# MoBA's scale, bias and maximum in one VectorE pass, its 1/sum scaling and some copies and fills on GpSimd

## The chip, the core and the metric

One core of one Trainium2 chip runs the whole program. The metric is the device time in microseconds of one execution, as the median of several. PE stands for TensorE, DVE for VectorE, ACT for ScalarE, POOL for GpSimd, SP for SyncE.

## What is computed

A decoder trunk of two layers on 256 tokens of width 1024, in float32. Each layer is a SwiGLU half-step, a mixing step, a cross-attention over 256 memory tokens, and a second SwiGLU half-step. The mixing step projects the normed tokens once and feeds the columns to an RWKV-7 time mix (8 heads of 64) and to MoBA, a block-sparse attention (8 heads of 64). With 256 tokens and blocks of 256 there is only each query's own block, so MoBA is a causal softmax attention with a bias by distance:

```python
s_own = jnp.einsum('bhqd,bhkd->bhqk', q_c, k_own).astype(f32) + bias_own.astype(f32)[None]
s_own = jnp.where(own_pos[None, :] <= q_pos[:, None], s_own, -jnp.inf)
...
probs = jax.nn.softmax(logits, axis=-1).astype(v.dtype)
```

where `q` has been multiplied by 64 ** -0.5 = 0.125.

## The kernel before

Every weight matmul is done in three terms of a high and a low half. `load` (L101) brings 1 MB of weights into one of two `raw` buffers by a DMA from SP's queue; `split` (L85) makes the high half on ACT (tile `whi`) and the low half on DVE (tile `wlo`, a subtraction with two inputs in SBUF), into five buffers each. PE consumes them in groups of 24 matmuls of 256 columns.

`mix` (L878) runs three things against each other: the generator `rwkv` (L560), the generator `moba` (L483), and projections of the memory tokens for the cross-attention (`late`, L928), which are the weight matmuls of this stretch. `rwkv` yields numbers, and `mix` hands out pieces of the others against them; the Tile scheduler then sets the order in which each engine's queue holds its instructions, and each engine works through its queue in that order.

`moba` has the steps `scores(h)` and then `values(h - 1)`, for 8 heads. For each head `scores` puts q k^T into a PSUM bank (`acc`, tile `mqk` as input) in two pieces, `t` = 0 (128 queries by 128 keys) and `t` = 1 (128 by 256). DVE multiplies by 0.125 and adds the bias `bp` (L511), takes the negated maximum (L516), ACT takes the exponential with its row sum (L517), DVE the reciprocal of the sums (L519), and ACT multiplies by it (L521, shown as L83). `values` transposes `lg` on PE in three parts (L530), copies them out on ACT (`mpT`), and multiplies by v. The bias table is made once by `moba_bias` (L472) and loaded per pair of heads by a DMA from POOL's queue (L492).

In `rwkv`, after the products `XB` of each half `cp` of the chunks, 32-row blocks are copied to `UD` (L691, ACT) and 16-row blocks to `UA` (L694, POOL); a transpose (`UT`, L699) and then 14 pairs of a product `pr` (L720) and a sum into `mb` (L722) on DVE invert small triangular matrices. The inverses become `M` and `W2` (L729); PE then multiplies `UA` by `M` (L762), and so on in 32 by 32 pieces. The zero parts of `G` (L613), `W` (L732) and of the first state `SV` (L752) are filled on DVE.

Of the kernel before, what the change touches and what calls it, by code (L numbers as in the profile page):

```python
# [11 lines left out]
AF = mybir.ActivationFunctionType  # L12
OP = mybir.AluOpType
AX = mybir.AxisListType

D = 1024
S = 256
# [9 lines left out]
NEG = -1e30  # L27
# [20 lines left out]
def body(tc, ctx, I, out):  # L48
    nc = tc.nc
# [7 lines left out]
    V = nc.vector  # L57
    A = nc.scalar
# [8 lines left out]
    def H(shape, dt=FT, name="h", tag="e"):  # L67
        return hp.tile(shape, dt, name=nm(name), tag=tag, bufs=HEAP[tag])

    def SM(shape, dt=FT, name="s", tag="sm"):  # L70
        return sp.tile(shape, dt, name=nm(name), tag=tag, bufs=SMALL.get(tag, 8))

    def BANK(tag):
        return ps.tile([128, 512], FT, name=nm(tag), tag=tag, bufs=BANKS[tag])

    def tt(out_, a, b, op):
        V.tensor_tensor(out=out_, in0=a, in1=b, op=op)  # L77

    def stt(out_, a, s, b, op0, op1):
        V.scalar_tensor_tensor(out_, a, s, b, op0=op0, op1=op1)  # L80

    def copy(out_, in_, **k):
        return A.activation(out_, in_, AF.Copy, **k)  # L83

    def split(hi, lo, src):  # L85
        c = copy(hi, src)
        tt(lo, src, hi.bitcast(FT), OP.subtract)
        return c.ins
# [4 lines left out]
    def mm(o, a, b, start=True, stop=True):  # L93
        nc.tensor.matmul(o, a, b, start=start, stop=stop, skip_group_check=True)  # L94
# [377 lines left out]
    def moba_bias():  # L472
        rel, oh = table
        u = SM([8, 384], name="u", tag="k2")
        V.memset(u[:, 256:384], NEG)
        p = BANK("pm")
        mm(p[0:8, 0:S], rel, oh)
        copy(u[:, 0:S], p[0:8, 0:S])
        nc.gpsimd.dma_start(scr_t, u)
        t = scr_t[:, :]  # L480
        nc.gpsimd.dma_start(scr_b, bass.AP(tensor=t.tensor, offset=t.offset, ap=[[0, 128], [1, 8 * 384]]))

    def moba(qT, kT, v, yT):  # L483

        scr = scr_b[:, :]
        cols = (slice(0, 128), slice(128, 384))
        probs, os = {}, {}

        def load_bias(p):
            if p < 4:  # L490
                bias[p] = SM([128, 2, S], name="bp", tag="k3")
                nc.gpsimd.dma_start(bias[p], bass.AP(  # L492
                    tensor=scr.tensor, offset=scr.offset + 2 * p * 384 + 127,
                    ap=[[8 * 384 - 1, 128], [384, 2], [1, S]]))

        bias = {}
        load_bias(0)
        yield 0.0

        def scores(h):  # L500
            p, e = divmod(h, 2)
            r = half(e)
            if e == 0:
                load_bias(p + 1)
            s = BANK("acc")
            for t in range(2):
                mm(s[:, cols[t]], qT[p // 2][r, p % 2, t * 128:(t + 1) * 128],
                   kT[p // 2][r, p % 2, 0:(t + 1) * 128])
            lg = SM([128, 384], name="lg", tag="k3")
            for t in range(2):  # L510
                stt(lg[:, cols[t]], s[:, cols[t]], 0.125, bias[p][:, e, 128 * (1 - t):S],  # L511
                    OP.mult, OP.add)
            m = SM([128, 2], name="m", tag="n2")
            z = SM([128, 2], name="z", tag="n2")
            for t in range(2):
                V.tensor_reduce(m[:, t:t + 1], lg[:, cols[t]], axis=AX.X, op=OP.max, negate=True)  # L516
                A.activation(lg[:, cols[t]], lg[:, cols[t]], AF.Exp, bias=m[:, t:t + 1],  # L517
                             accum_out=z[:, t:t + 1])
            V.reciprocal(z, z)  # L519
            for t in range(2):  # L520
                copy(lg[:, cols[t]], lg[:, cols[t]], scale=z[:, t:t + 1])  # L521
            probs[h] = lg

        def values(h):
            p, e = divmod(h, 2)
            r = half(e)
            lg = probs.pop(h)
            q = BANK("acc")[:, 0:384].rearrange("p (k t) -> p k t", k=3)
            for k in range(3):
                nc.tensor.transpose(q[:, k, :], lg[:, k * 128:(k + 1) * 128], ident)  # L530
            pT = SM([128, 3, 128], name="mpT", tag="k3")
            copy(pT, q)
            if e == 0:
                os[p] = BANK("acc")
            o = os[p]
            for t in range(2):
                for k in range(t + 1):
                    mm(o[r, t * 128:(t + 1) * 128], v[k][:, h * 64:h * 64 + 64], pT[:, t + k, :],
                       k == 0, k == t)
            if e:  # L540
                split(yT[0][:, p, :], yT[1][:, p, :], o[:, 0:S])

        for h in range(9):
            if h < 8:
                scores(h)
            if h:
                values(h - 1)
            yield 1.6
# [8 lines left out]
    def half(e):  # L557
        return slice(e * 64, e * 64 + 64)

    def rwkv(l, xT, yT):  # L560
# [26 lines left out]
        for j in range(2):  # L587
            for which in range(3):
                ac = BANK("pm").rearrange("p (c t) -> p c t", c=2)
                for c in range(2):  # L590
                    p = 2 * j + c
# [5 lines left out]
                for c in range(2):  # L597
                    p = 2 * j + c
                    if which == 2:
                        copy(G1[:, p, :], ac[:, c, :], scale=X(8, p))  # L600
                    else:
                        A.activation((sg, a)[which][:, p, :], ac[:, c, :], AF.Sigmoid,
                                     bias=P((P_W0, P_A0)[which], p))
# [5 lines left out]
        for p in range(4):  # L609
            V.tensor_tensor_scan(Lc[:, p, :], con[:, C_SCAN:C_SCAN + S], sg[:, p, :], 0.0,  # L610
                                 op0=OP.mult, op1=OP.add)
        G = H([128, 4, NCH, 65], name="G")
        V.memset(G[:, :, :, 0:1], 1.0)  # L613
        A.activation(G[:, :, :, 1:65], ch(Lc), AF.Exp, scale=-DECAY_C)
        Gi = H([128, 4, S], name="Gi")
        A.activation(Gi, Lc, AF.Exp, scale=DECAY_C)
# [56 lines left out]
        quads = [slice(32 * b, 32 * b + 32) for b in range(4)]  # L673
        UD = SM([128, 16, 4, 4, 2], name="UD", tag="k2")
        for c in range(NCH):
            cp, cc = divmod(c, 2)
            for e in range(2):
                hs, ho = half(e), half(1 - e)
                px = BANK("pm").rearrange("p (c t) -> p c t", c=4)
                for p in range(4):  # L680
                    mm(px[:, p, :], BK[cp][hs, cc, p, :], ZL[e][cp][hs, cc, p, :])
                tt(XB[cp][hs, cc], px[0:64], con[hs, None, C_MB:C_MB + 128].to_broadcast([64, 4, 128]),
                   OP.mult)
                tt(ZL[e][cp][ho, cc], px[64:128],
                   con[ho, None, C_MK:C_MK + 128].to_broadcast([64, 4, 128]), OP.mult)
                yield XY
            if cc:
                for b in range(4):
                    c0 = (b // 2) * 64 + (b % 2) * 32
                    z = XB[cp][quads[b], :, :, c0:c0 + 32]  # L690
                    copy(UD[quads[b], :, 2 * cp:2 * cp + 2].rearrange("p i n c b -> p (n c) b i"),  # L691
                         z.rearrange("p n c (b i) -> p (n c) b i", b=2))
                    r16 = slice(32 * b, 32 * b + 16)
                    nc.gpsimd.tensor_copy(UA[r16, cp * 8:cp * 8 + 8, 16:32],  # L694
                                          z[0:16, :, :, 16:32].rearrange("p n c t -> p (n c) t"))
# [11 lines left out]
        for c in range(NCH):  # L707
            cp, cc = divmod(c, 2)
# [6 lines left out]
        for i in range(14, -1, -1):  # L715
            n = 15 - i
# [12 lines left out]
            V.transpose(zz.rearrange("p n (b i) -> p i n b", b=2), ex.rearrange("p i b j -> p (i b j)"))  # L729
        W = H([128, 16, 64], name="W")  # L730
        for e in range(2):
            V.memset(W[e * 64 + 32:e * 64 + 64, :, 0:32], 0.0)  # L732
        SV = []
        pvt = []

# [13 lines left out]

        values(0)  # L750
        for e in range(2):
            V.memset(SV[0][half(e), :, e, 0, :], 0.0)  # L752
        hq = [slice(e * 64, e * 64 + 32) for e in range(2)]
        hr = [slice(e * 64 + 32, e * 64 + 64) for e in range(2)]
        for cp in range(2):
# [47 lines left out]
        for c in range(NCH):  # L803
            cp, cc = divmod(c, 2)
# [219 lines left out]
    first, scale = start()  # L1024
    gf = None
    for l in range(L):
        xT = [o[0] for o in ops[4 * l:4 * l + 4]]
        post = [o[1] for o in ops[4 * l + 1:4 * l + 5]]
        ffn(xT[0] if l else xT0, I["w_f1i"][l], I["w_f1o"][l], post[0], I["w_mixb"][l],
            *(() if l else (  # L1030
                {2: (bias_load,), 3: (aux_params,), 4: (mem_tokens,), 7: (moba_bias,), 9: (mem_norm,)}, first, scale)))
        kT, vx = mix(l, xT[1], post[1])
        xattn(l, xT[2], kT, vx, post[2], I["w_f2i"][l])
        if l == L - 1:
            gf = H([128, D], name="gf")
            nc.gpsimd.dma_start(gf, bass.AP(tensor=I["gfin"].tensor, offset=I["gfin"].offset,
                                            ap=[[0, 128], [1, D]]))
            V.tensor_scalar(gf, gf, RS, None, op0=OP.mult)
        ffn(xT[3], I["w_f2i"][l], I["w_f2o"][l], post[3], I["w_f1i"][l + 1] if l < L - 1 else None)
# [116 lines left out]
```

## Time and profile before

| | |
|---|---|
| median of 3 runs | 1313.62 us (1313.3 to 1314.08) |
| the profiled execution | 1309.71 us |
| its span in the trace | 1307.9 us |
| busy: PE, DVE, ACT, POOL | 1290.9, 919.2, 761.8, 63.0 us |
| granted clock of PE, mean | 0.998 |

The span runs from the first to the last instruction of the trace; the device time has 1.8 us around it. The MoBA part of the first layer lies at some 290 to 350 us of the span, that of the second layer at some 936 to 997 us, with the same instructions in the same order on PE. A matmul that starts while the one before it still runs is drawn overlapping, so what PE loses is read from the spacing of the starts as much as from its idle time.

### The profile page before, as it was taken

What the parts mean: (1) busy time and instruction counts of PE and PEld (TensorE: products, weight loads), DVE (VectorE), ACT (ScalarE), POOL (GpSimd) and SP (SyncE); (2) the same over time, 40 slices, a digit from 0 to 9 for tenths busy, and PEclk for the clock granted to TensorE, in tenths of its full rate; (3) what the DMA queues carried; (4) which work ended last, traced back from release to release, by engine and by line L of the source; (5) the groups of instructions that cost most, each with busy time, mean ns of one, the idle gap of its engine ahead of it and who ended that gap; (6) DMA issues with size and microseconds to landing.
All of it is one profiled execution on the core that took longest, in us unless ns stands there. A gap on an engine that the chain in (4) does not pass through costs nothing.

```text
span 1307.9 us, 21991 instructions
## 1 busy us (share of the span) xinstructions
PE 1290.9 (99%) x8710; PEld 1107.2 (85%) x8710; DVE 919.2 (70%) x1703; ACT 761.8 (58%) x1447; POOL 63.0 (5%) x69
## 2 busy tenths in 40 slices
PE   9999999999999999999999999999999999999997
PEld 7888888998878888888888888889887798888886
DVE  6797556797598676665576665658966976777744
ACT  6656437658656466554365554574785555665543
POOL 0080000020000000000000000000200000000000
PEclk9999999999999999999999999999999999999999
DMA  7867663333235335556545556443431455355552
GB/s 283 315 238 251 220 209 129 130 129 117 102 139 193 133 134 199 186 190 223 193 140 184 192 194 225 145 139 120 144 133 66 140 183 173 134 193 192 185 173 95
DMA packets 34422, 224.36 MB, mean 172 GB/s; under 512 B 4328, under 2 KB 4752, under 8 KB 9104
## 3 DMA queue, kind: packets, MB, share of 16 engines
q1 hardware_dynamic: 31344, 212.93, 46.6%
q0 software_dynamic: 2400, 9.45, 2.2%
q8 instruction: 68, 1.11, 0.4%
q10 hardware_dynamic: 576, 0.59, 0.1%
q14 instruction: 34, 0.28, 0.1%
HBM read 219.80 MB, written 4.73 MB: 172 GB/s over the span
## 4 chain that ended last, share of the span: by engine, by line
PE 82%; DVE 7%; ACT 6%; DMA 3%; issue 1%; SPq 0%; ACTq 0%
PE acc L94 75%; PE pm L94 5%; DMA raw<-in_w_f1i_dram 2%; DVE wlo L77 2%; ACT whi L83 1%; DVE ZL L77 1%; PE tr L199 1%; DVE XB L77 1%; DMA raw<-in_w_k_dram 1%; ACT lg L517 1%; ACT BT L83 1%; DVE wb L77 1%; ACT W L83 0%; ACT xt L83 0%; PE acc L530 0%
## 5 line engine op out<-in xcount | busy, mean ns | idle before, releaser
L94 PE MATMUL acc<-xt,whi 128*128 128x512 f32 (+1 forms) x2496 | 679.2, 343 | 0.6 <-ACT whi L83 0.4
L77 DVE TENSOR_TENSOR wlo<-raw,whi 128x1024 fp32r<-128x1024 f32 (+1 forms) x456 | 465.2, 1036 | 237.6 <-ACT whi L83 236.6
L83 ACT ACTIVATE whi<-raw 128x1024 fp32r<-128x1024 f32 (+1 forms) x456 | 404.2, 906 | 320.0 <-PE acc L94 212.3
L94 PE MATMUL acc<-xt,wlo 128*128 128x256 f32 x1888 | 530.2, 281 | 0.8 <-DVE wlo L77 0.8
L94 PEld LDWEIGHTS acc<-xt,whi 128*128 128x128 f32 x2496 | 431.2, 189 | 62.6 <-issue 2.4
L94 PEld LDWEIGHTS acc<-xt,wlo 128*128 128x128 f32 x1888 | 357.4, 189 | 3.5 <-DVE wlo L77 1.5
L94 PE MATMUL acc<-whi,hT 128*128 128x512 f32 x704 | 220.8, 393 | 0.0
L94 PEld LDWEIGHTS acc<-whi,hT 128*128 128x128 f32 x704 | 132.4, 188 | 30.1
L94 PE MATMUL acc<-wlo,hT 128*128 128x512 f32 x352 | 138.5, 393 | 0.0
L94 PEld LDWEIGHTS acc<-wlo,hT 128*128 128x128 f32 x352 | 66.2, 188 | 14.8
L77 DVE TENSOR_TENSOR z<-acc,z 128x256 f32<-128x256 f32 x160 | 66.9, 418 | 2.1 <-ACT z L83 2.1
L94 PE MATMUL acc<-wb,xt 128*128 128x512 f32 x240 | 62.0, 400 | 0.0
L83 ACT ACTIVATE z<-acc 128x256 f32<-128x256 f32 x160 | 58.5, 366 | 2.8 <-PE acc L94 2.8
L83 ACT ACTIVATE xt<-tr,par 128x128 fp32r<-128x128 f32 x112 | 38.3, 364 | 28.3 <-PE tr L199 15.3
L94 PE MATMUL acc<-whi,xt 128*128 128x512 f32 x160 | 53.2, 408 | 1.5 <-ACT whi L83 1.5
L94 PEld LDWEIGHTS acc<-wb,xt 128*128 128x128 f32 x240 | 43.3, 188 | 9.5 <-ACT xt L83 0.7
L83 ACT ACTIVATE hT<-z 128x256 fp32r<-128x256 f32 x80 | 32.4, 405 | 20.4 <-DVE z L77 20.4
L80 DVE SCALAR_TENSOR_TENSOR xt<-tr,par,xt 128x128 fp32r<-128x128 f32 x112 | 36.2, 347 | 8.3 <-ACT xt L83 8.2
L174 ACT ACTIVATE junk<-x 128x512 f32<-128x512 f32 x36 | 22.7, 632 | 33.0 <-DVE x L80 25.0
L77 DVE TENSOR_TENSOR z<-z,z 128x256 f32<-128x256 f32 x80 | 36.5, 456 | 7.3
L94 PE MATMUL acc<-whi,oT 128*128 128x512 f32 x128 | 40.3, 393 | 0.0
L77 DVE TENSOR_TENSOR hT<-z,hT 128x256 fp32r<-128x256 f32 x80 | 35.5, 443 | 3.2 <-ACT hT L83 3.2
(237 smaller groups left out, 1256.1 us busy)
## 6 DMA issues: line engine op xcount, KB each, us to landing
raw<-in_w_f2i_dram SPq DMA_DIRECT2D x44, 1024.0 KB, 4.8
raw<-in_w_f1i_dram SPq DMA_DIRECT2D x42, 1024.0 KB, 4.9
raw<-in_w_f1o_dram SPq DMA_DIRECT2D x22, 1024.0 KB, 4.9
raw<-in_w_mixa_dram SPq DMA_DIRECT2D x22, 1024.0 KB, 4.8
raw<-in_w_f2o_dram SPq DMA_DIRECT2D x22, 1024.0 KB, 4.8
raw<-in_w_k_dram SPq DMA_DIRECT2D x8, 1024.0 KB, 4.8
raw<-in_w_v_dram SPq DMA_DIRECT2D x8, 1024.0 KB, 5.1
raw<-in_w_mixo_dram SPq DMA_DIRECT2D x8, 1024.0 KB, 4.8
```

The costliest lines, as they stand in the source:

```text
L77: V.tensor_tensor(out=out_, in0=a, in1=b, op=op)
L80: V.scalar_tensor_tensor(out_, a, s, b, op0=op0, op1=op1)
L83: return A.activation(out_, in_, AF.Copy, **k)
L94: nc.tensor.matmul(o, a, b, start=start, stop=stop, skip_group_check=True)
L174: marks["square"] = A.activation(junk, xt[:, n * 512:(n + 1) * 512], AF.Square, scale=1.0 / 32.0, accum_out=ss[:, n:n + 1]).ins
L199: nc.tensor.transpose(p[:, k, :], xs[:, k * 128:(k + 1) * 128], ident)
L517: A.activation(lg[:, cols[t]], lg[:, cols[t]], AF.Exp, bias=m[:, t:t + 1], accum_out=z[:, t:t + 1])
```

## The change

Four edits. DVE does bias, scale and minimum of MoBA's logits in one instruction that writes the result and its row minimum; it computes (s + 8 bias) * -0.125, the negated logits, so the bias table is made 8 times as large, and the exponential takes them with scale -1. The multiplication by 1/sum goes from ACT to POOL. The `UD` copies of the first half (`cp` = 0) go from ACT to POOL. The fills of `G`, `W` and `SV` go from DVE to POOL.

```diff
-        copy(u[:, 0:S], p[0:8, 0:S])
+        copy(u[:, 0:S], p[0:8, 0:S], scale=8.0)
...
-            for t in range(2):
-                stt(lg[:, cols[t]], s[:, cols[t]], 0.125, bias[p][:, e, 128 * (1 - t):S],
-                    OP.mult, OP.add)
...
-                V.tensor_reduce(m[:, t:t + 1], lg[:, cols[t]], axis=AX.X, op=OP.max, negate=True)
-                A.activation(lg[:, cols[t]], lg[:, cols[t]], AF.Exp, bias=m[:, t:t + 1],
+                V.tensor_tensor_reduce(lg[:, cols[t]], s[:, cols[t]], bias[p][:, e, 128 * (1 - t):S],
+                                       -0.125, -NEG, OP.add, OP.min, m[:, t:t + 1])
+                A.activation(lg[:, cols[t]], lg[:, cols[t]], AF.Exp, bias=m[:, t:t + 1], scale=-1.0,
                              accum_out=z[:, t:t + 1])
             V.reciprocal(z, z)
             for t in range(2):
-                copy(lg[:, cols[t]], lg[:, cols[t]], scale=z[:, t:t + 1])
+                nc.gpsimd.tensor_scalar(lg[:, cols[t]], lg[:, cols[t]], z[:, t:t + 1], None, op0=OP.mult)
...
-        V.memset(G[:, :, :, 0:1], 1.0)
+        nc.gpsimd.memset(G[:, :, :, 0:1], 1.0)
...
-                    copy(UD[quads[b], :, 2 * cp:2 * cp + 2].rearrange("p i n c b -> p (n c) b i"),
-                         z.rearrange("p n c (b i) -> p (n c) b i", b=2))
+                    d = UD[quads[b], :, 2 * cp:2 * cp + 2].rearrange("p i n c b -> p (n c) b i")
+                    z4 = z.rearrange("p n c (b i) -> p (n c) b i", b=2)
+                    if cp:
+                        copy(d, z4)
+                    else:
+                        nc.gpsimd.tensor_copy(d, z4)
...
-            V.memset(W[e * 64 + 32:e * 64 + 64, :, 0:32], 0.0)
+            nc.gpsimd.memset(W[e * 64 + 32:e * 64 + 64, :, 0:32], 0.0)
...
-            V.memset(SV[0][half(e), :, e, 0, :], 0.0)
+            nc.gpsimd.memset(SV[0][half(e), :, e, 0, :], 0.0)
```

The scheduler gives other orders for it. Three places of it are shown; in both layers they read alike.

PE, first layer, from the scores of head 1 (`mqk`) on, before: `tr` is the transpose of RWKV's v, `lg_3019` the probabilities of head 0, `xt,whi` and `xt,wlo` the weight matmuls.

```order
L94 MATMUL acc_3094<-mqk_2037,mqk_2035 128x128
L94 MATMUL acc_3094<-mqk_2037,mqk_2035 128x256
L744 MATMUL tr_3133<-con,rkv_2124 128x128 x4
L530 MATMUL acc_3109<-con,lg_3019 128x128
L94 MATMUL acc_3043<-xt_2959,whi_3048 128x256 x2
L94 MATMUL acc_3043<-xt_2959,wlo_3049 128x256
L530 MATMUL acc_3109<-con,lg_3019 128x128 x2
```

Now:

```order
L94 MATMUL acc_3092<-mqk_2037,mqk_2035 128x128
L94 MATMUL acc_3092<-mqk_2037,mqk_2035 128x256
L528 MATMUL acc_3105<-con,lg_3019 128x128 x3
L746 MATMUL tr_3129<-con,rkv_2124 128x128 x4
L94 MATMUL acc_3041<-xt_2959,whi_3046 128x256 x2
L94 MATMUL acc_3041<-xt_2959,wlo_3047 128x256
```

The three transposes of head 0 stand directly behind the scores of head 1; before, the four of v stood ahead of them, and three weight matmuls between the first and the other two.

DVE, first layer, around the reciprocal of head 2 (`z_3265` before, `z_3259` now); `tr_3203`/`tr_3199` and `pm_3204`/`pm_3200` are the 32 by 32 products on PE that follow `M,UA`. Before:

```order
L729 STREAM_TRANSPOSE M_3119<-ex_3121 128x16x32
L728 TENSOR_SCALAR ex_3125<-mb_2974,con 128x16x16 x2
L519 RECIPROCAL z_3265<-z_3265 128x2
L77 TENSOR_TENSOR yl_2030<-acc_3115,yh_2029 128x256
L729 STREAM_TRANSPOSE W_3120<-ex_3125 128x16x32
```

Now (L513 is the fused instruction, with `m` alone the reading of its minimum):

```order
L731 STREAM_TRANSPOSE W_3116<-ex_3121 128x16x32
L513 ISA lg_3257,m_3258<-acc_3254,bp_3014 128x256
L513 ISA m_3258 128x1
L77 TENSOR_TENSOR yl_2030<-acc_3111,yh_2029 128x256
L77 TENSOR_TENSOR M_3115<-tr_3199,M_3115 32x256 x2
L77 TENSOR_TENSOR wlo_3671<-raw_3668,whi_3670 128x1024
L77 TENSOR_TENSOR W_3116<-pm_3200,W_3116 128x256
L517 RECIPROCAL z_3259<-z_3259 128x2
L77 TENSOR_TENSOR wlo_3673<-raw_3668,whi_3672 128x1024
```

The reciprocal of head 2 has moved behind the updates of `M` and `W` that wait for PE, and a `wlo` follows it at once.

POOL, first layer, from the fills to the probabilities of head 2; the numbers after `lg` are as above, and `bp_3252` is the bias of the third pair of heads.

```order
L754 MEMSET SV_3128 64x4x64 x2
L734 MEMSET W_3125 32x16x32 x2
L519 TENSOR_SCALAR lg_3019<-lg_3019,z_3021 128x128
L519 TENSOR_SCALAR lg_3019<-lg_3019,z_3021 128x256
L492 DMA bp_3252<-scr_b 128x2x256
L519 TENSOR_SCALAR lg_3095<-lg_3095,z_3097 128x128
L519 TENSOR_SCALAR lg_3095<-lg_3095,z_3097 128x256
L519 TENSOR_SCALAR lg_3257<-lg_3257,z_3259 128x128
L519 TENSOR_SCALAR lg_3257<-lg_3257,z_3259 128x256
```

Before, only the load of `bp` stood here on POOL.

## Rows read from the trace of the kernel before

**Rows 1.** The page, part 1: busy us (share of the span) xinstructions

```profile
PE 1290.9 (99%) x8710; PEld 1107.2 (85%) x8710; DVE 919.2 (70%) x1703; ACT 761.8 (58%) x1447; POOL 63.0 (5%) x69
```

**Rows 2.** Busy time by engine in the first layer's MoBA: us, PE, PEld, DVE, ACT, POOL

```profile
290.00:350.00 60.00, 58.48 (x885) 48.82 (x885) 40.24 (x100) 46.85 (x116) 2.96 (x4) 1.00 0.32 108
```

**Rows 3.** The tile lg: line engine op, duration ns min/median/max, forms

```profile
L80 DVE SCALAR_TENSOR_TENSOR lg<-acc,bp x32: 261/346/419, 292.0 to 988.2; 128x128 f32<-128x128 f32 x16, 128x256 f32<-128x256 f32 x16
L516 DVE TENSOR_REDUCE m<-lg x32: 263/336/423, 292.6 to 988.7; 128x1 f32<-128x128 f32 x16, 128x1 f32<-128x256 f32 x16
L83 ACT ACTIVATE lg<-lg,z x32: 386/448/502, 296.5 to 991.1; 128x128 f32<-128x128 f32 x16, 128x256 f32<-128x256 f32 x16
```

**Rows 4.** Timeline of PE at head 0: start, us, line op [idle before <-releaser]

```profile
295.09 0.92 PE L94 MATMUL acc<-mqk,mqk 64*128 64x128 f32 x4
295.94 0.66 PE L744 MATMUL tr<-con,rkv 128*128 128x128 f32 x4
296.97 0.33 PE L530 MATMUL acc<-con,lg 128*128 128x128 f32 x1 [0.37 <-ACT lg L83]
297.05 0.48 PE L94 MATMUL acc<-xt,whi 128*128 128x256 f32 x2
297.49 0.38 PE L530 MATMUL acc<-con,lg 128*128 128x128 f32 x2
```

**Rows 5.** Timeline of DVE, the same stretch

```profile
293.07 0.22 DVE L77 TENSOR_TENSOR pr<-mb,ub 128x64 f32<-128x64 f32 x1
294.72 0.48 DVE L732 MEMSET W<- 32x512 f32 x1 [0.16 <-issue]
295.71 0.17 DVE L519 RECIPROCAL z<-z 128x2 f32<-128x2 f32 x1 [0.23 <-ACT lg L517]
298.40 0.30 DVE L722 TENSOR_REDUCE mb<-pr 128x12 f32<-128x144 f32 x1
```

**Rows 6.** Timeline of ACT, the same stretch

```profile
290.09 4.71 ACT L83 ACTIVATE BT<-tr 128x256 f32<-128x256 f32 x12
294.70 0.39 ACT L517 ACTIVATE lg<-lg,m 128x128 f32<-128x128 f32 x1
296.53 0.79 ACT L83 ACTIVATE lg<-lg,z 128x128 f32<-128x128 f32 x2
```

**Rows 7.** Instructions by shape on POOL: xcount | busy us, mean ns

```profile
L386 POOL TENSOR_SCALAR memG<-memT,par 128x256 f32<-128x256 f32 x16 | 23.1, 1456 | 0.1
L570 POOL TENSOR_SCALAR bo<-con,par 128x128 f32<-128x128 f32 x8 | 4.7, 593 | 52.4 <-PE tr L199 52.4
```

**Rows 8.** Timeline of POOL and DVE where GpSimd scales the memory tokens

```profile
83.89 0.94 POOL L386 TENSOR_SCALAR memG<-memT,par 128x256 f32<-128x256 f32 x1
83.89 6.31 POOL L386 TENSOR_SCALAR memG<-memT,par 128x256 f32<-128x256 f32 x4
84.12 1.34 DVE L77 TENSOR_TENSOR wlo<-raw,whi 128x1024 fp32r<-128x1024 f32 x1 [1.32 <-ACT whi L83]
86.00 1.21 DVE L77 TENSOR_TENSOR wlo<-raw,whi 128x1024 fp32r<-128x1024 f32 x1
```

**Rows 9.** Timeline of PE at heads 2 and 5

```profile
310.27 0.40 PE L94 MATMUL acc<-xt,whi 128*128 128x256 f32 x2
310.50 0.28 PE L94 MATMUL acc<-xt,wlo 128*128 128x256 f32 x1
310.99 0.43 PE L94 MATMUL acc<-mpT,mv 128*64 128x128 f32 x2 [0.21 <-ACT mpT L83]
312.11 0.69 PE L94 MATMUL tr<-M,XB 32*32 32x32 f32 x30
333.28 0.87 PE L94 MATMUL acc<-mpT,mv 128*64 128x128 f32 x6 [0.24 <-ACT mpT L83]
```

**Rows 10.** The tiles UD and UT: duration ns min/median/max, first and last start

```profile
L83 ACT ACTIVATE UD<-XB x16: 644/675/695, 268.3 to 926.8; 32x256 f32<-32x256 f32 x16
L699 DVE STREAM_TRANSPOSE UT<-UD x2: 699/700/701, 281.7 to 928.0; 128x512 f32<-128x512 f32 x2
```

## The prediction

> **What bounds the kernel now.** I read the page's busy times first: PE is busy 99% of the span and POOL 5% [rows 1]. The reader is to see that no other engine's busy time is worth anything by itself: a microsecond taken from DVE or ACT counts only where PE waits for them. So I went to the one stretch that the change touches, MoBA beside RWKV, and asked for the busy time by engine: of 60 us PE is idle 1.5 [rows 2]. Then I read PE's timeline there for waits on the softmax, then the timelines of DVE and ACT for what made them, and last POOL's rows for what its instructions cost. Over 0.2% of this kernel is 2.6 us, about what a measurement can tell from no change; both layers run the same stretch, so that is 1.3 us a layer. PE's clock is granted in full throughout, so clock plays no part.
>
> PE's waits on MoBA in a layer are few. At head 0 it waits 0.37 us for `lg` [rows 4]. At heads 2 and 5 it waits for `mpT`, ACT's copy of the transposed probabilities: idle 0.21 and 0.24 us [rows 9]. Drawn idle time understates this, since matmuls overlap: two matmuls start 0.23 apart, 0.12 each, but 0.49 us lies before the `mpT` matmul, so that wait is 0.37 [rows 9], and the other is about 0.4 in proportion. In all some 1.2 us a layer, and no gain can be much larger.
>
> **The change part by part**, for one layer.
>
> *The fused instruction.* For head 0 two additions and two maxima fill DVE from 292.0 to 293.07 [rows 3, 5]. No row shows the fused instruction. It cannot be below the additions alone, about half of that, 0.5; with two readings of the minimum and no saving it is 1.07 or more. I take 0.85, nearer the upper end, because a short instruction on DVE still takes 0.17 [rows 5]. On PE's path this gives nothing at head 0: ACT is in its twelve `BT` copies until 294.70 and the exponential follows them [rows 6], a cover of 1.6 us, which would also hide a fused pair that cost a microsecond more. The factor 8 on the bias is part of one copy that is there already: nothing.
>
> *Fills and early copies.* `W`, `SV` and `G` are filled by DVE beside its matrix inversion, 0.48 us for one half of `W` [rows 5]; on POOL they lie ahead of `lg` of head 0, which needs its reciprocal three microseconds later. They are covered. If POOL were late, `lg` of head 0 would be too. Four `UD` copies, 0.68 each on ACT [rows 10], go to POOL between its `UA` copies. `UT`, which needs them, starts 13 us after the first [rows 10], so even at 1.5 us each they are hidden. What DVE is relieved of makes `M` some 1 us earlier, and PE asks for it earlier by the new order, so I book no gain.
>
> *The scaling on POOL* is what counts. ACT does the two pieces of a head in 0.79 [rows 6], between 0.39 and 0.50 each [rows 3]. POOL's nearest rows are the same kind of instruction at the same shapes: 0.593 for 128x128 and 1.456 for 128x256 [rows 7]. The second mean holds delays: the first of the `memG` pieces took 0.94, although a `wlo` began 0.23 after it, and the four together 6.31, so the three behind it 1.8 each [rows 8]. A piece that begins while DVE is in a `wlo` (1.21 [rows 8]) waits for its end; a piece already running does not. So a head costs 0.59 + 0.94 = 1.53, 0.74 more than on ACT, plus up to 1.2 where its start falls into a `wlo`.
>
> *Head 0.* The reciprocal is at 295.71 now [rows 5]. In the new order five pairs of `pr` and its sum stand ahead of it; a pair takes from 0.44 to 0.60 [rows 5], with gaps 0.57 on average, so 2.85 from 292.85: it starts at 295.7 to 295.95 and ends at 296.0. POOL then ends the second piece at 297.6. PE is free at 295.94 and, in the new order, has nothing ahead of these transposes. At 297.49 it used to start its last two transposes, with four transposes of v (0.5 with the turn) and three weight matmuls (0.44) already done [rows 4]. Now it starts them at 297.6 without: behind by 0.1 + 0.5 + 0.44, **1.1 us**. This includes the old wait of 0.37.
>
> *The load of `bp`* for the third pair stands behind head 0's pieces on POOL, and in front of head 1's. It waits for PE's reading of head 0 as it did before; head 1's reciprocal comes later than that, and its first reader is the scores of head 4, three heads on. Nothing.
>
> *Head 1.* A `wlo` follows its reciprocal, so POOL begins 1.1 late. PE has 24 weight matmuls (2.9), v's transposes, one `values` (0.8 [rows 9]) and the scores of head 2 (0.85 [rows 4]) to do first, 5 us in all. Covered by a few tenths.
>
> *Head 2.* Its reciprocal stands behind the updates of `M` and `W`, and they wait for PE's 32 by 32 products. From the end of these, PE has ten weight matmuls (1.3 with the turn), sixteen small products (0.7 [rows 9]) and the scores of head 3 (0.85) until it wants `lg`: 2.9. DVE still has the rest of a `wlo`, the update of `W` and the reciprocal, an estimate of 1.9, and POOL 1.53: 3.4. Wait 0.5. The `wlo` right behind the reciprocal starts before POOL does, so the piece may wait for it and the wait be 1.6. I take **1.0**, between the ends.
>
> *Heads 3 to 7* have 2 us and more between the scaling and PE's transposes, and the extra 0.74 to 1.9 fits.
>
> *Given back.* ACT is free of 0.79 a head, so `mpT` comes in time at heads 2 and 5: **-0.8**. PE's order has fewer changes between weight matmuls and small ones, each about 0.08 (the first pair behind `lg` takes 0.32, to the next start, where two take 0.24): some four fewer, **-0.3**.
>
> The sum is 1.1 + 1.0 - 0.8 - 0.3 = +1.0 us a layer, **+2.0 us** in all. The profiled execution took 1309.7 (span 1307.9 and 1.8 around it), 3.9 below the median of the runs, 1313.6; the sum goes on top of either, so I predict **1315.6**. With head 2 between its ends it is 1314.6 to 1316.8.
>
> **The rivals.**
>
> *POOL is in time* (faster). If the pieces run at their bare price and the reciprocal of head 0 is early enough, or PE's stalls are shorter than counted, the old waits vanish and nothing replaces them: -0.5 (head 0, with overlap) - 0.8 - 0.3, that is -1.6 a layer, 1310.4. For it: POOL is idle. Against: PE's order leaves nothing ahead of head 0's transposes, and 1.53 against 0.79 is in the rows. It decides if `lg` of head 0 is ready before 296.5.
>
> *POOL is held more* (slower). Running pieces are also held by two-input instructions of DVE, `pr` among them. Then head 0 is 0.6 later, head 1 waits 1.1 and head 2 1.6: 1.7 + 1.1 + 1.6 - 1.1 = +3.3 a layer, 1320.2. For it: the mean of 1.456. Against: the 0.94 of a piece that had a `wlo` beside it.
>
> *DVE is held by POOL.* If a running piece stopped DVE's two-input instructions, the pieces of heads 0 and 1 would push the inversion and `M` back by up to 2.0 us (0.94 twice and a small one), of which some 0.5 is slack: +1.5 a layer, 1318.6. The row shows 1.34 for the `wlo` that began under a running piece, only 0.13 over 1.21 [rows 8]. The Trainium skill, page "SBUF — State Buffer", section "SBUF: two separate sides", states that whichever of the two starts first keeps the shared ports for its whole instruction and the other is fully blocked. That rule would have it this way, and would hold no piece that runs; the trace agrees for pieces that begin late and does not for DVE.
>
> *The fused instruction fuses nothing* or costs a microsecond more per head: three of them stand ahead of `M`, so PE would wait some 2 us more at `M,UA`: 1319.6.
>
> **How the numbers follow.** Forecast 0.46, POOL in time 0.15, POOL held more 0.17, DVE held 0.12, no fusion 0.10. Within 0.2% means 1311.0 to 1316.2. Two thirds of the forecast's own spread lies there, and the cases mix: half a stall at head 0 with the rest given back is no change. Faster 0.14, same 0.45, slower 0.41. The range from 1311.0 to 1320.0 leaves out most of the first rival and the far ends of the others, 0.2 together.
>
> **What would show it.** PE's timeline with a wait of 1.5 us at head 0's transposes, released by POOL, in both layers; a second, of 0.5 to 1.6, at head 2; none on `mpT`. POOL's rows for the scaling at 0.6 and 0.9 to 1.2. The fused pair with its readings below 1.07 for a head. It is wrong if head 0's transposes start before 296.5, or if PE waits at `M,UA`.

## The result: 0.7% slower, and four times the forecast loss

| | before | changed kernel |
|---|---|---|
| median of 4 executions each, us | 1313.46 (1311.89 to 1314.08) | 1321.82 (1318.49 to 1323.68) |
| ratio, 95% interval | | 1.0071 [1.0059, 1.0083] |
| profiled execution, span, us | 1309.71, 1307.9 | 1323.68, 1321.9 |
| mean granted TensorE clock of the profiled execution | 0.998 | 0.994 |

The loss is 8.4 us where +2.0 was forecast; 1321.82 lies outside the range. The page of the changed kernel, parts 1 and 2, answers to [rows 1]:

```profile
PE 1299.8 (98%) x8710; PEld 1113.3 (84%) x8710; DVE 910.8 (69%) x1693; ACT 747.3 (57%) x1407; POOL 100.4 (8%) x119
...
PEclk9999999998999999999999999999989999999999
```

POOL, DVE and ACT did what the change says: POOL +37 us, DVE -8, ACT -15. What the forecast had no place for is that PE itself is busy 8.9 us longer with the same 8710 matmuls. The row of the granted clock says why: it has two slices under 9 tenths, one in each layer's MoBA.

The changed kernel's tile `lg` (duration ns min/median/max), against [rows 3]:

```profile
L513 DVE CUSTOM_DVE_ANT_0 lg<-acc,bp x32: 274/343/422, 293.8 to 1000.2; 128x128 f32<-128x128 f32 x16, 128x256 f32<-128x256 f32 x16
L519 POOL TENSOR_SCALAR lg<-lg,z x32: 605/922/1902, 298.0 to 1003.2; 128x128 f32<-128x128 f32 x16, 128x256 f32<-128x256 f32 x16
```

And its tile `m`, the reading of the minimum that follows each fused instruction:

```profile
L513 DVE DVE_READ_ACCUMULATOR2_ANT m<- x32: 73/83/85, 294.1 to 1000.5; 128x1 f32 x32
```

The fused instruction costs what one addition did (median 343 against 346) plus a reading of 83 ns; the maximum is nearly free. The scaling takes 605 to 1902 ns on POOL where ACT took 386 to 502.

PE's timeline, at head 0 (answers to [rows 4]) and at head 2 (to [rows 9]):

```profile
297.02 0.92 PE L94 MATMUL acc<-mqk,mqk 64*128 64x128 f32 x4
298.64 0.33 PE L528 MATMUL acc<-con,lg 128*128 128x128 f32 x1 [0.70 <-POOL lg L519]
299.65 0.44 PE L528 MATMUL acc<-con,lg 128*128 128x128 f32 x2 [0.68 <-POOL lg L519]
...
312.19 0.92 PE L94 MATMUL acc<-mqk,mqk 64*128 64x128 f32 x4
313.13 0.33 PE L528 MATMUL acc<-con,lg 128*128 128x128 f32 x1
314.76 0.44 PE L528 MATMUL acc<-con,lg 128*128 128x128 f32 x2 [1.30 <-POOL lg L519]
...
315.89 0.63 PE L94 MATMUL acc<-xt,whi 128*128 128x256 f32 x2
316.31 0.41 PE L94 MATMUL acc<-xt,wlo 128*128 128x256 f32 x1
```

The forecast waits are there, with the releaser it named. The last two rows are the surprise: from the start of two 256-column matmuls to that of the next it is 0.42, where it was 0.23 in [rows 9]. The windows behind head 2 (us from : to, length, then busy time and count of PE, PEld (the loading of weights into PE), DVE, ACT, POOL, granted clock, DMA share, GB/s); the first line answers to [rows 2]:

```profile
290.00:350.00 60.00, 56.93 (x817) 48.26 (x815) 35.10 (x95) 39.33 (x95) 16.79 (x20) 0.94 0.31 112
310.00:314.00 4.00, 3.44 (x76) 2.63 (x63) 3.64 (x7) 2.61 (x7) 1.52 (x2) 1.00 0.00 0
314.00:316.00 2.00, 1.24 (x8) 1.03 (x9) 0.47 (x4) 1.94 (x7) 0.95 (x2) 0.90 0.46 115
316.00:318.00 2.00, 2.00 (x36) 1.71 (x35) 0.17 (x1) 0.67 (x4) 1.96 (x3) 0.50 0.99 414
318.00:320.00 2.00, 2.00 (x10) 2.00 (x10) 0.00 (x0) 0.71 (x2) 0.09 (x1) 0.50 0.36 133
320.00:322.00 2.00, 2.00 (x9) 1.45 (x9) 0.00 (x0) 0.00 (x0) 0.00 (x0) 0.50 0.01 2
322.00:324.00 2.00, 2.00 (x73) 1.82 (x74) 0.00 (x0) 0.93 (x1) 0.00 (x0) 0.89 0.00 0
```

Behind the wait at head 2, PE is granted half its clock (1.2 of 2.4 GHz) until about 322.4, and is busy all that time. The missing shares of these windows add up to 0.20 + 3 x 1.00 + 0.22 = 3.4 us of clock. The second layer repeats it (0.89, 0.50 three times, 0.91 from 966 to 976). The Trainium skill, page "TensorE: Matmul & The Clock Gate", Part 1, states that the activity monitor behind the gate sets only the half or the full rate; the rows agree, and 0.89 to 0.91 are windows in which it changed.

So each layer's cost can be read between two fixed places: from the first products of `ZL` by `BK` to the start of the last head's transposes, first of the kernel before, then of the changed one (PE's timeline):

```profile
260.74 1.71 PE L94 MATMUL pm<-ZL,BK 64*128 64x128 f32 x16
...
347.30 0.49 PE L530 MATMUL acc<-con,lg 128*128 128x128 f32 x3
```

```profile
262.56 1.71 PE L94 MATMUL pm<-ZL,BK 64*128 64x128 f32 x16
...
353.19 0.49 PE L528 MATMUL acc<-con,lg 128*128 128x128 f32 x3
```

86.56 and 90.63: +4.07, and +3.99 in the second layer (86.74 and 90.73), 8.1 us in all beside the 8.4 between the medians. Below, "the stage" is this stretch; in every profile it holds the same 360 weight matmuls. The two profiled executions are 14.0 us apart, and the other 5.9 lie outside the stages, 4.1 of them between and behind the two, where the same weight matmuls run a little slower for some 100 us (0.353 us a pair in place of 0.346). Why is not known: in the changed kernel's two profiles 1140.6 and 1141.2 us lie outside the stages, in all the others 1133.4 to 1136.9. The medians leave little room for it: the profiled execution of before was 3.8 us under its median, and both of the changed kernel were the longest of their runs.

### The profile page after: what moved, and what is told of

Read it like the earlier page. It is cut to its first block, busy times and chain, and to the rows that moved or that the text cites. A ratio compares the mean times of both kernels' runs of the same rounds, so it can differ in the third digit from the quotient of the medians.

```text
span 1321.9 us, 22036 instructions
## 1 busy us (share of the span) xinstructions
PE 1299.8 (98%) x8710; PEld 1113.3 (84%) x8710; DVE 910.8 (69%) x1693; ACT 747.3 (57%) x1407; POOL 100.4 (8%) x119
## 5 line engine op out<-in xcount | busy, mean ns | idle before, releaser
L94 PE MATMUL acc<-xt,whi 128*128 128x512 f32 (+1 forms) x2496 | 686.3, 345 | 0.6 <-ACT whi L83 0.5
```

## The experiments

The theories at the start: T1, the scaling on GpSimd; T2, the fused instruction or the order it brings; T3, the early copies and fills; T4, that the half clock comes from the order of the small matmuls and not from a wait. T5 came later. Kernels were timed beside the one before on the same chip, so ratios are compared. The clock is the lowest and highest mean granted clock of a kernel's executions (the kernel before: 0.997 to 0.999).

| kernel | median, us | before, us | ratio, 95% interval | stage, layers 1 and 2 | clock |
|---|---|---|---|---|---|
| act_scale | 1307.99 | 1310.94 | 0.9977 [0.9967, 0.9988] | 85.55, 85.51 | 0.997-0.999 |
| pool_scale_only | 1313.71 | 1310.94 | 1.0017 [1.0005, 1.0029] | 90.06, 88.24 | 0.995-0.999 |
| head2_act | 1310.42 | 1310.94 | 0.9996 [0.9985, 1.0006] | 87.65, 87.75 | 0.996-0.999 |
| head2_filled | 1314.98 | 1310.94 | 1.0035 [1.0023, 1.0046] | 87.63, 87.52 | 0.996-0.999 |
| dve_scale | 1307.95 | 1311.72 | 0.9973 [0.9960, 0.9986] | 85.15, 85.36 | 0.998-0.999 |
| fused_only | 1309.50 | 1311.72 | 0.9985 [0.9972, 0.9997] | 85.60, 85.58 | 0.994-0.999 |
| heads012_act | 1308.41 | 1311.72 | 0.9976 [0.9966, 0.9985] | 84.92, 84.81 | 0.998-0.999 |
| changed_again | 1319.59 | 1312.36 | 1.0061 [1.0044, 1.0078] | 91.97, 90.52 | 0.991-0.993 |
| both_filled | 1316.63 | 1312.36 | 1.0039 [1.0024, 1.0055] | 88.16, 92.36 | 0.996-0.998 |
| head0_act | 1307.88 | 1312.36 | 0.9968 [0.9955, 0.9980] | 85.45, 85.44 | 0.998-0.999 |
| fills_only | 1310.50 | 1312.36 | 0.9990 [0.9979, 1.0001] | 86.44, 86.28 | 0.998-0.999 |
| all_gpsimd_reordered | 1310.94 | 1312.01 | 0.9996 [0.9986, 1.0006] | 87.95, 87.89 | 0.994-0.999 |

### Which part loses

In the changed kernel, the scaling alone taken back:

```diff
-                nc.gpsimd.tensor_scalar(lg[:, cols[t]], lg[:, cols[t]], z[:, t:t + 1], None, op0=OP.mult)
+                copy(lg[:, cols[t]], lg[:, cols[t]], scale=z[:, t:t + 1])
```

**act_scale.**

> The changed kernel with the scaling by 1/sum back on ScalarE, nothing else undone. Theory (T1): the loss is the scaling on GpSimd, late for TensorE at heads 0 and 2, and at head 2 the wait is followed by half the granted clock. Then the time is 1311.5 to 1314.5 us, no stretch behind head 2 has a granted clock near 0.50, and the waits on lg at head 2 are under 0.3 us each. Rivals: the fused maximum on VectorE or the order it brings (T2), or the early copies and fills on GpSimd (T3): then the time stays at 1320 to 1323 us.

**pool_scale_only**, this edit the other way round in the kernel before:

> The kernel before with only the scaling by 1/sum moved to GpSimd. T1: slower, 1318 to 1323 us, if the wait at head 2 is again followed by half the clock, and 1315 to 1317 us if it waits and the clock holds (the order around head 2 is not the same as in the changed kernel). T2 or T3: 1312.5 to 1314.5 us.

**fused_only**, the kernel before with the fused instruction, the factor 8 on the bias and the sign in the exponential:

```diff
...
-                stt(lg[:, cols[t]], s[:, cols[t]], 0.125, bias[p][:, e, 128 * (1 - t):S],
-                    OP.mult, OP.add)
...
-                V.tensor_reduce(m[:, t:t + 1], lg[:, cols[t]], axis=AX.X, op=OP.max, negate=True)
+                V.tensor_tensor_reduce(lg[:, cols[t]], s[:, cols[t]], bias[p][:, e, 128 * (1 - t):S],
+                                       -0.125, -NEG, OP.add, OP.min, m[:, t:t + 1])
...
```

> The kernel before with only the fused scale, bias and maximum on VectorE. T1 (the scaling on GpSimd is the loss): 1312 to 1314 us. T2 (the fused instruction or the order it brings is the loss): 1318 to 1322 us.

**fills_only**, the kernel before with the `UD` copies of the first half and the fills of `G`, `W` and `SV` on GpSimd:

> The kernel before with only the early copies and the zero and one fills on GpSimd. T1: nothing that TensorE waits for moves, within 1.5 us of the kernel before. T3: 4 us slower or more.

T2 and T3 fall as causes by themselves. Without the scaling the rest of the change gains 0.23%; the fused instruction alone gains 0.15%; the fills alone cannot be told from nothing. The scaling alone loses 0.17%. The scaling alone lost less than in the changed kernel, so the loss needs the rest of the change beside it, which sets another order: in the profile of pool_scale_only PE waits for GpSimd at heads 0 and 1 but not at head 2, and the clock fell once, in the first layer, behind a stop of 1.39 us at `M,UA` for which no releaser is shown. The kernel before ran 1 to 2.5 us faster on these chips than in the runs of the result, so the ratios decide, not the absolute times expected (by these alone the 1313.71 of pool_scale_only would have spoken for T2 or T3). With the scaling back, the stage is 5.1 us a layer shorter than the changed kernel's (85.55 against 90.63).

### Is it head 2, and is it the idle time?

**head2_act**, the changed kernel with `if h == 2` sending the scaling to ScalarE:

> The changed kernel with the scaling of head 2 alone on ScalarE. T1: the waits of head 0 stay (0.9 and 0.9 us over the usual spacing), those of head 2 go, and the clock stays at 1.00 behind head 2: 1315 to 1317 us. If head 0 carried as much as head 2: 1317 to 1319 us. T2 or T3: 1320 to 1323 us. If the low clock came from the order of TensorE's small matmuls and not from the wait (T4), the clock is still 0.50 behind head 2 and the time is above 1318 us.

It is level with the kernel before, better than expected, so most of the loss hangs on head 2. The clock held behind head 2, as expected, but half the clock came behind head 0 instead, in both layers. Windows of this kernel, first layer (columns as above):

```profile
298.00:300.00 2.00, 1.43 (x8) 1.43 (x9) 2.00 (x6) 1.81 (x7) 0.94 (x2) 0.71 0.04 8
300.00:302.00 2.00, 2.00 (x11) 2.00 (x11) 2.00 (x5) 1.99 (x3) 1.90 (x2) 0.50 0.43 98
```

Its waits at head 0 are those of the changed kernel (drawn 0.69 and 0.68), and up to head 2 PE's order is the same. So the same wait is followed by half the clock in one execution and not in another.

**head2_filled**, the wait left in place and PE given work in it, whose results nobody reads:

```diff
...
             for k in range(3):
+                if k == 1 and h == 2:
+                    for _ in range(7):
+                        mm(bank[:, 384:512], ident, ident)
                 nc.tensor.transpose(q[:, k, :], lg[:, k * 128:(k + 1) * 128], ident)
```

> The changed kernel with seven matmuls of identity by identity (fp32, 128x128), whose results nobody reads, between the first and the second transposes of head 2, where TensorE waits for GpSimd. The wait for GpSimd stays as long, but TensorE works in it. T1, in the form that the idle time brings the clock down: the granted clock stays at 1.00 behind head 2, and the time is 1315 to 1318 us. T4 (the order of small matmuls brings it down) or T2 or T3: the clock falls as in the changed kernel and the time is 1320 to 1324 us.

PE's timeline of this kernel at head 2 (the seven matmuls are drawn as 14), and its windows there:

```profile
312.50 0.33 PE L532 MATMUL acc<-con,lg 128*128 128x128 f32 x1
312.66 1.73 PE L94 MATMUL acc<-con 128*128 128x128 f32 x14
314.23 0.38 PE L532 MATMUL acc<-con,lg 128*128 128x128 f32 x2
```

```profile
314.00:316.00 2.00, 1.90 (x42) 1.49 (x40) 0.17 (x1) 1.94 (x8) 0.96 (x3) 1.00 0.83 225
316.00:318.00 2.00, 1.93 (x15) 1.76 (x16) 0.00 (x0) 0.64 (x3) 1.38 (x2) 1.00 0.97 406
```

From the first transpose to the second it is 1.73 us here and 1.63 in the changed kernel: GpSimd is as late as ever. But the clock stays at 1.00, in both layers, and the stage takes 87.63 in place of 90.63. That prices the half clock behind head 2 at **3.0 us** in the first layer and 3.2 in the second (90.73 against 87.52), and leaves +1.07 and +0.78 over the kernel before for everything else. This is read from one profile of each kernel. By the ratios this kernel is 0.26 to 0.36% better than the changed one, 3.4 to 4.7 us, with an interval of 2 to 3 us either way, so 6.2 for both layers stands at the upper end. The median, 1314.98, lies at the lower edge of the expected 1315 to 1318, but 4.0 us over the kernel before on its chip, with executions up to 1319.38 at a clock of 0.996: head 0's waits are open as before. PE's order is that of the changed kernel up to the wait; behind it, the 32 small `W,TB` stand in one run and not in two, so this kernel does not rule out T4 by itself.

**both_filled**, four more such matmuls ahead of the first and four ahead of the second transposes of head 0:

> The changed kernel with idle matmuls in both places where TensorE waits for GpSimd: four before the first and four before the second transposes of head 0, seven between the first and second of head 2. T1 (the idle time at these two heads brings the clock down): a mean granted clock of 0.998 or more in every execution, no stretch below 0.99 in either layer, and what is left is the two waits, about 1.0 us a layer over the kernel before: 0.5 to 3.5 us above it, with a spread of 5 us at most. If the low clock of some executions of the kernel filled at head 2 alone came from somewhere else than head 0, clocks of 0.996 and times 5 us above the fastest are here too.

A miss. No clock fell behind head 0 or head 2 in either layer, but the added matmuls also shifted the scheduler's order, and PE stopped somewhere new. PE's timeline in the second layer, and the windows:

```profile
956.86 0.69 PE L94 MATMUL pm<-W,T 32*32 32x32 f32 x57
959.50 0.25 PE L94 MATMUL pm<-W,T 32*32 32x32 f32 x5 [1.96 <-issue]
```

```profile
958.00:960.00 2.00, 0.50 (x7) 0.46 (x8) 0.41 (x3) 0.00 (x0) 1.50 (x2) 0.96 0.00 0
960.00:962.00 2.00, 2.00 (x10) 1.67 (x9) 0.65 (x2) 0.83 (x3) 0.00 (x0) 0.50 0.04 8
```

In the middle of a run of small matmuls PE issues nothing for 2 us, with no releaser that the profile shows, and half the clock follows. It does not settle what it was made for, but it shows the fall behind idle time for which the profile names no other engine.

### Why GpSimd is late at head 2

**changed_again**, the changed kernel once more:

> The changed kernel itself once more, so that it stands beside the others on one chip and with more executions. If the two stretches of half clock belong to its waits at head 2, they are there again in both layers, the mean granted clock of its executions is 0.992 to 0.995, and it takes 8 to 10.5 us more than the kernel before. If they were chance, the clock is 0.997 or more in a good part of the executions and those take 1311 to 1315 us.

**head0_act**, the changed kernel with the scaling of head 0 alone on ScalarE, heads 1 to 7 left on GpSimd:

```diff
-                nc.gpsimd.tensor_scalar(lg[:, cols[t]], lg[:, cols[t]], z[:, t:t + 1], None, op0=OP.mult)
+                if h == 0:
+                    copy(lg[:, cols[t]], lg[:, cols[t]], scale=z[:, t:t + 1])
+                else:
+                    nc.gpsimd.tensor_scalar(lg[:, cols[t]], lg[:, cols[t]], z[:, t:t + 1], None, op0=OP.mult)
```

> The changed kernel with the scaling of head 0 alone on ScalarE. T1: the waits of head 0 go (1.1 us a layer), those of head 2 and the half clock behind them stay: 6 to 9 us above the kernel before. If only the two heads together bring the clock down: no stretch of half clock, and at most 2 us above the kernel before.

changed_again came 7.2 us over the kernel before, a little under the 8 to 10.5 expected, with the half clock behind head 2 in both layers again and clocks of 0.991 to 0.993 throughout. head0_act was the surprise: T1 wanted 6 to 9 us over the kernel before, and it is 4.5 us under. It beats both kernels. Behind head 2 its PE mixes small and weight matmuls as the changed kernel does (two `W,TB` at 311.88, thirty from 312.49, weights between), at full clock, so T4 falls too. Its POOL, PE and DVE timelines at head 2:

```profile
308.00 2.24 POOL L522 TENSOR_SCALAR lg<-lg,z 128x128 f32<-128x128 f32 x2 [5.53 <-DVE z L517]
```

```profile
305.13 0.63 PE L94 MATMUL tr<-T,W 32*32 32x32 f32 x29 [0.27 <-DVE m L513]
...
310.55 0.92 PE L94 MATMUL acc<-mqk,mqk 64*128 64x128 f32 x4
311.40 0.55 PE L531 MATMUL acc<-con,lg 128*128 128x128 f32 x3
```

```profile
306.52 0.86 DVE L77 TENSOR_TENSOR M<-tr,M 32x256 f32<-32x256 f32 x2
307.41 0.42 DVE L77 TENSOR_TENSOR W<-pm,W 128x256 f32<-128x256 f32 x1
307.75 0.15 DVE L517 RECIPROCAL z<-z 128x2 f32<-128x2 f32 x1
```

And the same place in the changed kernel, POOL, PE, DVE and ACT:

```profile
312.48 2.24 POOL L519 TENSOR_SCALAR lg<-lg,z 128x128 f32<-128x128 f32 x2 [7.25 <-DVE z L517]
```

```profile
308.99 0.66 PE L94 MATMUL tr<-T,W 32*32 32x32 f32 x29
```

```profile
309.73 0.86 DVE L77 TENSOR_TENSOR M<-tr,M 32x256 f32<-32x256 f32 x2 [0.47 <-PE tr L94]
310.63 1.23 DVE L77 TENSOR_TENSOR wlo<-raw,whi 128x1024 fp32r<-128x1024 f32 x1
311.88 0.43 DVE L77 TENSOR_TENSOR W<-pm,W 128x256 f32<-128x256 f32 x1
312.23 0.15 DVE L517 RECIPROCAL z<-z 128x2 f32<-128x2 f32 x1
312.65 1.27 DVE L77 TENSOR_TENSOR wlo<-raw,whi 128x1024 fp32r<-128x1024 f32 x1 [0.27 <-ACT whi L83]
```

```profile
309.65 0.50 ACT L515 ACTIVATE lg<-lg,m 128x256 f32<-128x256 f32 x1
```

GpSimd takes 2.24 us for head 2 in both. In head0_act it ends at 310.24 and PE comes for `lg` at 311.40, 1.2 us later; in the changed kernel it ends at 314.72, 1.5 us after PE has begun to wait. In both, the reciprocal stands behind the updates of `M` and `W`, which need PE's products of `T` by `W` (`tr<-T,W` and `pm<-W,T`). So count from the first of these products. GpSimd ends 5.1 us behind it in head0_act and 5.7 in the changed kernel, where a `wlo` of 1.23 us stands between the two updates on DVE. PE comes for `lg` 6.3 us behind it in head0_act and 4.1 in the changed kernel, where it has less to do in between. ScalarE's order differs too (in the changed kernel the second exponential starts at 309.65, 3.4 us behind the first), but the reciprocal did not wait for it: it ended at 310.15, and the reciprocal started at 312.23. The scheduler's order differs: with head 0's scaling on GpSimd it lays PE's transposes of head 0 straight behind the scores of head 1 and, after the scores of head 2, puts the transposes of head 1 and ten weight matmuls ahead of the products `M,UA`, which stand between the two pieces of these scores in head0_act; all that hangs on the products (`T`, `W`) comes later, and less of PE's own work is left between them and the transposes of head 2. That gave T5: the order makes head 2 late, not GpSimd's own time.

**all_gpsimd_reordered** leaves all eight scalings on GpSimd and moves only source lines: `values(0)` of `rwkv` (the transposes of v and their copies), with its definition, and the fill of `SV` now stand ahead of the inversion loop.

```diff
...
+        values(0)
+        for e in range(2):
+            nc.gpsimd.memset(SV[0][half(e), :, e, 0, :], 0.0)
         for i in range(14, -1, -1):
...
-        values(0)
-        for e in range(2):
-            nc.gpsimd.memset(SV[0][half(e), :, e, 0, :], 0.0)
         hq = [slice(e * 64, e * 64 + 32) for e in range(2)]
```

> The changed kernel with the scaling of all eight heads still on GpSimd, but with the four transposes of v and the copies that follow them written ahead of the inversion loop. The scheduler then puts three weight matmuls between the scores of head 1 and the transposes of head 0, and 19 (not 10) ahead of the transposes of M by XB before the scores of head 3. Theory T5: the loss at head 2 and the half clock come from the order in which TensorE, ScalarE and VectorE meet the late scaling of head 0, and not from GpSimd's own time at head 2. Then the waits at head 2 and the half clock go although GpSimd still scales there: 4 us under to 2 us above the kernel before, mean granted clock 0.998 or 0.999. T1 in its first form (GpSimd's time is too long at head 2, whatever the order): waits of 1 us or more there, half the clock in most executions, 5 to 10 us above the kernel before.

POOL's and PE's timelines of this kernel at head 2:

```profile
311.84 2.23 POOL L519 TENSOR_SCALAR lg<-lg,z 128x128 f32<-128x128 f32 x2 [6.74 <-DVE z L517]
```

```profile
309.61 0.66 PE L94 MATMUL tr<-T,W 32*32 32x32 f32 x29
...
314.74 0.55 PE L528 MATMUL acc<-con,lg 128*128 128x128 f32 x3
```

GpSimd's 2.23 us are unchanged; it ends at 314.07, and PE's transposes at 314.74 wait for nothing. Counted from the products of `T` by `W`, GpSimd ends 4.5 us behind them and PE comes at 5.1. T5 holds: within 0.1% of the kernel before, where the changed kernel is 0.6 to 0.7% slower. But head 0 still waits (drawn 0.41 and 0.57), and in this profile half the clock followed there in both layers; the half clock was expected to go, and a mean clock of 0.998 was not reached in every execution.

### Other places for the scaling

**heads012_act**, heads 0 to 2 on ScalarE and 3 to 7 on GpSimd:

> The changed kernel with the scaling of heads 0 to 2 on ScalarE and that of heads 3 to 7 on GpSimd. T1: only the scalings at which TensorE has little other work are late, so 1311.5 to 1314.5 us, within 1 us of the kernel with all the scaling back on ScalarE, and no half clock. If GpSimd is also late at heads 3 to 7: 1 to 4 us above that kernel.

**dve_scale**, the scaling on VectorE:

> The changed kernel with the scaling by 1/sum on VectorE, right behind the reciprocal. T1: no engine is waited for between the reciprocal and the scaling, so the waits at heads 0 and 2 go; 1311 to 1314 us, no half clock behind head 2. T2 or T3: 1320 to 1323 us. If VectorE is too late with the added work (about 0.3 us for each head's scaling), a new wait of TensorE for VectorE at heads 1 to 3 and 1315 to 1318 us.

Both gain, 0.24% and 0.27%, and in neither did the clock fall. head0_act, heads012_act, act_scale and dve_scale have overlapping intervals: any of them beats both kernels, and the runs don't rank them. The stage of heads012_act is the shortest, 0.6 to 0.7 us a layer under act_scale: with ScalarE freed at heads 3 to 7, PE no longer waits for `mpT` at head 5 (a drawn 0.56 us in act_scale, no wait in the changed kernel).

## Why the prediction was wrong

**The step that failed** is a sentence of the first part: "PE's clock is granted in full throughout, so clock plays no part." That was read from the kernel before, where PE hardly waits, and carried to a kernel for which the same text forecast waits of 1.5 us. Half the clock behind head 2 costs 3.0 and 3.2 us in the two layers by the profiles, 6.2 of the 8.4 us (3.4 to 4.7 by the ratios). None of the rivals had it.

**The sum without the clock came out right, in part by luck.** +1.0 a layer was forecast; head2_filled, which has the late GpSimd and the full clock, shows +1.07 and +0.78 in its two layers. But two terms were off and cancel: the wait at head 2 was 0.5 longer than taken, and 0.5 to 0.8 more was given back.

- *Head 0, +1.1.* From the scores of head 1 to the last two transposes it was 297.49 - 295.09 = 2.40 us [rows 4], with the transposes of v (0.5) and three weight matmuls (0.44) done; it is now 299.65 - 297.02 = 2.63 without them: 1.17.
- *Head 1, covered.* No wait was drawn there, though POOL took 3.68 us for its two pieces.
- *Head 2, +1.0 between 0.5 and 1.6.* The wait is 1.63 less the usual 0.11 from one transpose to the next, 1.52, near the upper end, for the reason named there: the second piece lies beside a `wlo`. What the text did not see is that the order of PE and VectorE around this wait comes from the scaling of head 0, and that keeping head 0 on ScalarE undoes it.
- *Heads 3 to 7 fit; given back, -1.1.* The waits on `mpT` at heads 2 and 5 are gone, but only the second by ScalarE's free time: with the fused instruction alone the wait at head 2 is gone too, and that at head 5 is longer (drawn 0.56). ScalarE freed at heads 3 to 7 gives back 0.6 to 0.7 (heads012_act against act_scale). Together with the gain of the next point, heads012_act, where PE waits for GpSimd nowhere, has a stage 1.64 and 1.93 under that of before.
- *The fused instruction.* 0.85 a head was taken for the pair; it is 0.56 (from 293.84 to the next instruction at 294.40, which is drawn beside the second reading). It was said to give nothing on PE's path, at head 0 rightly, but fused_only's stage is 1.0 and 1.2 us shorter than that of before. I booked no gain for an earlier `M`; where exactly this gain arises was not taken apart.
- *Fills and copies: nothing.* fills_only agrees, [0.9979, 1.0001].

**The rivals.** "POOL is in time" fell at its own sign: head 0's last transposes wait for POOL until 299.65, where the sign was 296.5 (298.3 with the 1.8 us by which the changed kernel's stage starts later). "POOL held more" gave 1320.2, nearest in time, but by waits at head 1 that are not there. "The fused instruction fuses nothing" is refuted by its 343 ns, and PE does not wait at `M,UA`. "DVE is held by POOL": the `wlo` beside POOL's scaling at head 2 took 1.27 against 1.21 [rows 8], while POOL's pair took 2.24 against 1.51 at its shortest, so POOL is the one that is held. The Trainium skill's page "SBUF — State Buffer", section "SBUF: two separate sides", would block DVE fully behind a running piece; the trace again agrees only for pieces that begin late.

## What to carry to other kernels

Where TensorE runs at full clock with hardly a gap, a new wait of 1.5 us can cost more than its length: look at the granted clock behind each wait that a change makes, and put a price on the fall in the forecast. When a change moves a step to a slower engine, try first which single place pays for it: here one head of eight kept on ScalarE turned a loss of 0.6% into a gain of 0.3%. A late engine at one place may be an order made at another: compare the same instruction's duration and what stands ahead of it in the kernel that waits and the one that doesn't.

## What the hardware showed that was not expected

- Half the clock followed the wait at head 2 in 4 of 4 layers of the changed kernel's two profiles, and the two waits at head 0 (each 0.6 to 0.9 us beyond the usual spacing) in 5 of 12 layers of the six profiles that have them, and the changed kernel's own two profiles differ there. In the seven profiles without a wait for GpSimd at heads 0 to 2, the kernel before among them, it was not seen in either layer's MoBA (both_filled, whose waits are filled, counts in neither group). One execution of fused_only, without a profile, took 1315.22 us at a clock of 0.994; where it fell is not known. What decides at head 0 stays open, and no run has the wait at head 2 without those at head 0 some 13 us ahead of it, so that it is enough by itself is not shown.
- PE stops inside or right behind runs of 32 by 32 matmuls without a releaser: 1.96 us in both_filled and 1.39 in the first layer of pool_scale_only, with half the clock behind both; 1.00 in the second layer of pool_scale_only, and 0.33 and 0.50 at `M,UA` in the two layers of the kernel before, at full clock. The traces hold a hint: the DMA queue q8 moves 68 blocks of 16 KB in the kernel before, one for each 256 of PE's 17420 matmuls and weight loads, and each of these five stops ends 1.2 to 1.5 us behind the end of such a block (958.21 and 959.50 in both_filled, 319.49 and 320.85 in pool_scale_only). That PE waited there for its own instructions was not tested.
- Seven matmuls in the wait at head 2, whose results nobody reads, kept the clock at 1.00 there; they did not shorten the wait.
